# An S5 state scan with a fourth tree level, shared between VectorE and GpSimd, and its coefficients built later

## The chip, the cores and the metric

The kernel runs on one core of one Trainium2 chip. TensorE (PE) does the matrix products and transposes, VectorE (DVE), ScalarE (ACT) and GpSimd (POOL) work element by element, and SyncE (SP) issues the DMAs. The metric is the device time of one execution in microseconds: the median of several runs.

## The reference, cut to what matters

The program is a trunk of two layers over 2048 positions of width 1024. The even layer makes one projection and feeds stick-breaking attention and an S5 branch; the odd layer is a chunked gated linear attention. The change concerns the S5 branch and the two gate projections beside it:

```python
h = rms_norm(x, even_norm_g[i])
proj = h @ even_w_in[i]                      # q | k | v | gate A | S5 input u | gate B
...
lam_bar = jnp.exp(lam * dt)                  # 32 groups x 64 complex states
b_bar = ((lam_bar - 1.0) / lam)[..., None] * bmat
bu = lax.complex(jnp.einsum('gnp,blgp->blgn', b_bar.real, uf),
                 jnp.einsum('gnp,blgp->blgn', b_bar.imag, uf))
_, hstate = lax.associative_scan(combine, (a, bu), axis=1)   # h_t = lam_bar h_(t-1) + bu_t
y = (jnp.einsum('gpn,blgn->blgp', c_re, hstate.real)
     - jnp.einsum('gpn,blgn->blgp', c_im, hstate.imag) + d_skip * uf)
```

## The kernel before

All large products are made in two parts of reduced precision: `split` (L314 and L315) has ACT round a tile to `hi` and another engine take the rest, `lo`; each product is then three matmuls (`mm3`, L67 to L69). `sh` and `sl` are the parts of activations, `whi` and `wlo` those of weights.

The normalized and transposed input stands in four tiles hT0 to hT3 of 512 positions each (`m` = 0 to 3). `Norm.tiles` makes one tile of 128 positions: a sum of squares on ACT (L95), `nms` and `nrs` on POOL (L54, L56), `h` on DVE (L97), transposes on PE (`ntp`, L102), and copies to hT. The gate projections are sweeps over the four blocks (`first_gates`, `gates`): 96 matmuls of 512 columns a block into `gps`, then a sigmoid on ACT and a product on DVE into `sg` (L365). The PSUM ring that `gps` and `ups` share holds four tiles.

The S5 recurrence works on chunks of 8 positions, so that 256 chunks remain. Its coefficients are made once, in `s5_setup`: powers of lam_bar (`er`, L199 on POOL, then small DVE steps `p`), W by a chain of complex products (`cmul`, six instructions each, L228 to L233, on POOL), its transposes (L246) to `bin_d`; G by 8 `cmul`s that build on one another (on DVE); from G and `bz` the matrices K0 by 128 small matmuls (L290), copied to `kt` (L296, L297), reloaded as `ka` (8 DMAs, L302) and stored to `k0_d` (16 DMAs, L305), the DMAs all on SP's queue. `between(m)` runs between the blocks of the first gate sweep: norm tiles of the next block, and at m=1 `coefficients()`.

`s5_in` takes the 32 groups in two halves `cb`, each as 8 pairs of groups: for each `cb`, for two halves of the sequence and each of 8 offsets j, it splits hT with a stride of 8 elements (two splits of 128x512, `b` = 0 and 1), makes 24 matmuls of 256 columns into `ups`, and copies them to `U` (ACT, L487). Then it transposes U, multiplies by W (`bp`, L500) and copies the result to `H` (DVE, L504): 8 pairs x real and imaginary x 256 chunks for each `cb`. `scan_up` combines neighbours at distances 1, 2 and 4 with the powers `pwr` and `pwi` (three tree levels; `cplx_acc` is five instructions, `ca`, `cb` twice, `ca`, `H`, L458 to L462, on DVE), and then a chain of 31 steps of four POOL instructions of 128x16 (L530 to L533) runs over every eighth chunk. `scan_down` brings the results back down the tree. After `s5_in` comes the gate sweep of the next 512 columns (the "512 gates"), then `s5_out` (`yps`), and further gates.

Each engine works through its own queue in order. The order in which the queues are filled is set by a scheduler from the program and its dependencies, not by the text order alone, so the code's stages interleave on an engine.

Of the kernel before, what the change touches and what calls it, by code (L numbers as in the profile page):

```python
# [155 lines left out]
def s5_setup(e, room, lr, li, dt, sn, sh, b_re, b_im, c_re, c_im, dsk, bin_d, k0_d, co_d):

# [6 lines left out]
    V = nc.vector  # L164
    MU, AD, SU = ALU.mult, ALU.add, ALU.subtract

    e.pwr = [e.cst.tile([P, NI], F32, name=f"pwr{a}") for a in range(4)]
    e.pwi = [e.cst.tile([P, 2, NI], F32, name=f"pwi{a}") for a in range(4)]
    with e.pool("s5s", 1, "right") as s, e.pool("s5t", 2, "right") as s2, e.pool("s5w", 1, "right") as sw, \
            e.pool("s5p", 2, "right", PSUM) as pp:  # L170
        def tt(a, b, op, name):
# [38 lines left out]


        pr, pi = br, bi
        for a in range(6):
# [4 lines left out]
            if a >= 2:
                V.tensor_copy(e.pwr[a - 2], pr)
                V.tensor_scalar(e.pwi[a - 2][:, 0, :], pi, -1.0, None, MU)  # L220
                V.tensor_copy(e.pwi[a - 2][:, 1, :], pi)
# [37 lines left out]
                V.tensor_scalar(G[a][q, :, 0, :], ps[q].rearrange("q h (i r p) -> q (h i) r p", r=2, p=16)[:, :, r],  # L259
                                -1.0 if a else 1.0, None, MU)  # L260
# [189 lines left out]
def cplx_acc(e, tp, dst, src, lv, n, eng):  # L450

    nI = dst.shape[2]
    i0 = e.i0
    a = tp.tile([P, 2, nI, n], F32, tag="ca", name="ca")
    b = tp.tile([P, 2, nI, n], F32, tag="cb", name="cb")
# [2 lines left out]
    eng.tensor_tensor(a, src, pr, ALU.mult)  # L458
    for r in range(2):
        eng.tensor_tensor(b[:, r], src[:, 1 - r], pi[:, r].unsqueeze(2).to_broadcast([P, nI, n]), ALU.mult)  # L460
    eng.tensor_tensor(a, a, b, ALU.add)
    eng.tensor_tensor(dst, dst, a, ALU.add)  # L462


def s5_in(e, pn, hT, w_in, bin_d, u_d, H, lo_eng):

    nc, tc = e.nc, e.tc
    with e.pool("u_b", 2, "right") as ub, e.pool("u_1", 1, "right") as u1, e.pool("u_p", 2, "right", PSUM) as up:
        ws = pn.load(w_in, 4 * D, 512, lo_eng)
        for cb in range(2):  # L470
            nc.vector.memset(H[cb][:, :, :, 0:1], 0.0)
            bt = u1.tile([P, 2, 8, P], F32, tag="bt", name="bt")
            for a in range(2):
                nc.sync.dma_start(out=bt[:, a], in_=bin_d[a, cb * 8:cb * 8 + 8].rearrange("i j q -> j i q"))
            for half in range(2):
                U = ub.tile([P, 16, T8, 16], F32, tag="U", name="U")
                for j in range(T8):
                    hi = pn.s.tile([P, KD, P], F32R, tag="sh", name="sh")
                    lo = pn.s.tile([P, KD, P], F32R, tag="sl", name="sl")
                    for b in range(2):  # L480
                        split(nc, hi[:, :, b * 64:(b + 1) * 64], lo[:, :, b * 64:(b + 1) * 64],
                              hT[half * 2 + b][:, :, j::T8], lo_eng)
# [5 lines left out]
                for g4 in range(4):  # L488
# [8 lines left out]
                    for i in range(2):  # L497
                        for par in range(2):
                            for a in range(2):
                                nc.tensor.matmul(bp[par * 64:par * 64 + 64, a, i, :],  # L500
                                                 lhsT=bt[:, a, g4 * 2 + i, par * 64:par * 64 + 64],
                                                 rhs=us[:, i * 2 + par, :], start=True, stop=True)
                    i0 = g4 * 2
                    nc.vector.tensor_copy(H[cb][:, :, i0:i0 + 2, 1 + half * P:1 + (half + 1) * P], bp)  # L504
# [5 lines left out]
def scan_up(e, H, i1, tp, t2):  # L510

    B = H[:, :, :, 1:]
    V, G = e.nc.vector, e.nc.gpsimd
    for i0 in range(0, 8, 4):
        e.i0 = i1 + i0
        b = B[:, :, i0:i0 + 4]
        for h in range(2):
            c = slice(h * 128, h * 128 + 128)
            bh = b[:, :, :, c]
            cplx_acc(e, tp, bh[:, :, :, 1::2], bh[:, :, :, 0::2], 0, 64, V)  # L520
        cplx_acc(e, tp, b[:, :, :, 3::4], b[:, :, :, 1::4], 1, 64, V)
        cplx_acc(e, tp, b[:, :, :, 7::8], b[:, :, :, 3::8], 2, 32, V)
    ii = slice(i1, i1 + 8)
    pr = e.pwr[3][:, ii].unsqueeze(1).to_broadcast([P, 2, 8])
    pi = e.pwi[3][:, :, ii]
    for c in range(15, NC, 8):
        src = B[:, :, :, c - 8]
        a = t2.tile([P, 2, 8], F32, tag="sa", name="sa")
        b = t2.tile([P, 2, 8], F32, tag="sb", name="sb")
        G.tensor_tensor(a, src, pr, ALU.mult)  # L530
        G.tensor_tensor(b, src[:, ::-1], pi, ALU.mult)
# [1 line left out]
        G.tensor_tensor(B[:, :, :, c], B[:, :, :, c], a, ALU.add)  # L533


def scan_down(e, H, i1, tp):

    B = H[:, :, :, 1:]
    V = e.nc.vector
    for i0 in range(0, 8, 4):  # L540
        e.i0 = i1 + i0
        b = B[:, :, i0:i0 + 4]
        cplx_acc(e, tp, b[:, :, :, 11::8], b[:, :, :, 7:NC - 1:8], 2, 31, V)
        cplx_acc(e, tp, b[:, :, :, 5::4], b[:, :, :, 3:NC - 1:4], 1, 63, V)
        cplx_acc(e, tp, b[:, :, :, 2:128:2], b[:, :, :, 1:127:2], 0, 63, V)
        cplx_acc(e, tp, b[:, :, :, 128::2], b[:, :, :, 127:NC - 1:2], 0, 64, V)
# [686 lines left out]
def tile_trunk(ctx, tc, x, even_norm_g, even_w_in, sb_q_norm_g, sb_k_norm_g, s5_lambda_re, s5_lambda_im, s5_log_dt,  # L1233
# [17 lines left out]
    V, G = nc.vector, nc.gpsimd  # L1251

    def coefficients():
        s5_setup(e, room, *angles, s5_b_re[0], s5_b_im[0], s5_c_re[0], s5_c_im[0],
                 s5_d[0], bin_d, k0_d, co_d)

    with ExitStack() as st:
# [12 lines left out]
        first, angles, room = first_gates(e, pn, nrm, hT, w0, 3 * D, zs_d, lambda: s5_angles(  # L1270
            e, sap, s5_lambda_re[0], s5_lambda_im[0], s5_log_dt[0]))
# [5 lines left out]
        H = [hpool.tile([P, 2, 8, NC + 1], F32, name=f"H{cb}") for cb in range(2)]  # L1277
# [96 lines left out]
```

## Time and profile before

| | |
|---|---|
| median of 3 runs | 2872.51 us (2870.74 to 2874.99) |
| profiled execution | 2872.48 us, span of the core 2870.8 us |
| mean granted clock of PE | 0.989 |
| POOL busy | 1197.6 us (42%), 1321 instructions |
| HBM | 129.36 MB read, 74.65 MB written, 71 GB/s |

Times in the profile count from the start of the span. A row of a group of instructions gives line, engine, operation, `out<-in` with the shapes of both, the count, busy time and mean duration in ns, then the idle time of that engine just before these instructions and what ended it. A row of a timeline gives start, duration, engine, line and operation. A wait is put down to what ended it last.

Places in time: the first gate sweep with the norms and coefficients takes the first 150 us, `ups` of cb=0 and cb=1 run from 150 to 276 us, the 512 gates and the scan to about 395 us, the next gates and `yps` come behind.

### The profile page before, as it was taken

The numbers are of one execution on the slowest core, as the hardware profiler recorded it, in microseconds if no ns is written. First come the engines' busy times: TensorE is split into PE (matmuls) and PEld (weight loads), VectorE is DVE, ScalarE is ACT, GpSimd is POOL, SyncE is SP. The second block draws the span as 40 slices with busy tenths as digits, with TensorE's granted clock in tenths as the row PEclk, the third lists the DMA queues.
The fourth block names the chain that finished last, engine by engine and source line by source line (L and its number), as shares of the span: only waits on it lengthen the run. The fifth ranks groups of instructions, "written<-read, shape, count | busy, mean of one in ns | idle before, by whom it ended". The sixth has DMA issues, their size and how long they took to land.

```text
span 2870.8 us, 46525 instructions
## 1 busy us (share of the span) xinstructions
PE 2765.3 (96%) x17433; PEld 2496.6 (87%) x17433; DVE 1719.9 (60%) x2733; ACT 1365.0 (48%) x2988; POOL 1197.6 (42%) x1321
## 2 busy tenths in 40 slices
PE   6989979899999999999999999999999999999999
PEld 6788767889999999999899978887788999999887
DVE  7768965657676857685767783223345566565521
ACT  4576224446555655555555552223345566565310
POOL 7201821366665665666556730000023455455300
PEclk9999989999999999999999999999999999999999
DMA  5532136511110111111112124332131021121343
GB/s 170 153 81 75 58 94 201 173 44 43 29 41 27 45 29 40 29 41 27 41 27 73 58 72 143 104 103 86 56 99 41 31 67 54 36 78 60 125 137 114
DMA packets 246898, 215.69 MB, mean 75 GB/s; under 512 B 46256, under 2 KB 215568, under 8 KB 246160
## 3 DMA queue, kind: packets, MB, share of 16 engines
q1 hardware_dynamic: 246096, 210.62, 24.2%
q8 instruction: 137, 2.24, 0.3%
q10 hardware_dynamic: 576, 2.10, 0.2%
q14 instruction: 89, 0.73, 0.1%
HBM read 129.36 MB, written 74.65 MB: 71 GB/s over the span
## 4 chain that ended last, share of the span: by engine, by line
PE 78%; DVE 7%; POOL 4%; issue 4%; ACT 3%; DMA 3%; SPq 1%; ACTq 0%; POOLq 0%; DVEq 0%
PE av L807 6%; PE pp L68 6%; PE pp L67 6%; PE pp L69 6%; PE ops L69 5%; PE ops L68 5%; PE ops L67 5%; PE w L796 4%; PE gps L67 3%; PE gps L68 3%; PE gps L69 3%; PE qk L67 2%; PE qk L69 2%; PE qk L68 2%; PE z L68 2%
## 5 line engine op out<-in xcount | busy, mean ns | idle before, releaser
L719 POOL TENSOR_TENSOR sl<-hT,sh 128x1024 fp32r<-128x1024 f32 x128 | 322.2, 2518 | 343.0 <-ACT sh L718 304.8
L67 PE MATMUL pp<-whi,sh 128*128 128x384 f32 x1024 | 357.4, 349 | 0.7 <-ACT whi L314 0.6
L68 PE MATMUL pp<-wlo,sh 128*128 128x384 f32 x1024 | 351.1, 343 | 0.2
L69 PE MATMUL pp<-whi,sl 128*128 128x384 f32 x1024 | 348.0, 340 | 0.0
L790 DVE TENSOR_TENSOR_SCAN pt<-om,pt,zero 128x513 f32<-128x513 f32 x192 | 279.2, 1477 | 38.0 <-ACT om L788 37.3
L67 PE MATMUL gps<-sh,whi 128*128 128x512 f32 (+1 forms) x672 | 252.8, 389 | 23.1 <-DVE sg L365 20.3
L68 PE MATMUL gps<-sl,whi 128*128 128x512 f32 (+1 forms) x672 | 259.1, 386 | 3.5 <-DVE sl L315 3.5
L69 PE MATMUL gps<-sh,wlo 128*128 128x512 f32 (+1 forms) x672 | 256.5, 384 | 0.0
L799 DVE TENSOR_TENSOR tl<-w,th 128x512 fp32r<-128x512 f32 (+2 forms) x320 | 186.6, 599 | 95.5 <-ACT th L798 93.6
L798 ACT ACTIVATE th<-w 128x512 fp32r<-128x512 f32 (+2 forms) x320 | 163.9, 535 | 149.3 <-PE w L796 148.8
L315 DVE TENSOR_TENSOR sl<-hT,sh 128x1024 fp32r<-128x1024 f32 (+1 forms) x148 | 172.1, 1186 | 50.4 <-ACT sh L314 48.2
L69 PE MATMUL ops<-woh,ol 128*128 128x512 f32 x496 | 196.8, 397 | 0.7 <-DVE ol L315 0.7
L68 PEld LDWEIGHTS pp<-wlo,sh 128*128 128x128 f32 x1024 | 193.6, 189 | 3.8 <-POOL wlo L315 1.7
L67 PEld LDWEIGHTS pp<-whi,sh 128*128 128x128 f32 x1024 | 193.5, 189 | 3.6 <-ACT whi L314 1.3
L68 PE MATMUL ops<-wol,oh 128*128 128x512 f32 x496 | 196.2, 395 | 0.0
L67 PE MATMUL ops<-woh,oh 128*128 128x512 f32 x496 | 195.6, 395 | 0.0
L69 PEld LDWEIGHTS pp<-whi,sl 128*128 128x128 f32 x1024 | 193.3, 189 | 2.6
L790 DVE TENSOR_TENSOR_SCAN pt<-om,zero 128x129 f32<-128x129 f32 (+3 forms) x128 | 158.8, 1262 | 56.8 <-ACT om L788 56.2
L314 ACT ACTIVATE sh<-hT 128x1024 fp32r<-128x1024 f32 (+1 forms) x148 | 155.8, 1093 | 62.0 <-PE gps L69 32.5
L788 ACT ACTIVATE om<-z 128x512 f32<-128x512 f32 (+2 forms) x320 | 167.0, 538 | 37.6 <-PE z L784 22.7
L718 ACT ACTIVATE sh<-hT 128x1024 fp32r<-128x1024 f32 x128 | 135.5, 1059 | 90.8 <-PE pp L68 90.5
L796 PE MATMUL w<-ident,pt 128*128 128x128 f32 x1088 | 165.2, 273 | 8.6 <-DVE tl L799 6.0
(327 smaller groups left out, 8001.7 us busy)
## 6 DMA issues: line engine op xcount, KB each, us to landing
zs_d<-sg SPq DMA_DIRECT2D x80, 256.0 KB
o<-o_d SPq DMA_DIRECT2D x80, 256.0 KB
xt<-in_x_dram SPq DMA_DIRECT2D x28, 512.0 KB
r<-in_even_w_in_dram SPq DMA_DIRECT2D x64, 192.0 KB
zs<-zs_d SPq DMA_DIRECT2D x64, 128.0 KB
o_d<-ot SPq DMA_DIRECT2D x64, 128.0 KB
r<-in_odd_w_in_dram SPq DMA_DIRECT2D x64, 128.0 KB
zs<-zs_d SPq DMA_DIRECT2D x32, 256.0 KB
```

The costliest lines, as they stand in the source:

```text
L67: nc.tensor.matmul(out, lhsT=lhi, rhs=rhi, start=start, stop=False)
L68: nc.tensor.matmul(out, lhsT=lhi, rhs=rlo, start=False, stop=False)
L69: return nc.tensor.matmul(out, lhsT=llo, rhs=rhi, start=False, stop=stop)
L314: a = nc.scalar.activation(hi, src, AF.Copy)
L315: b = lo_eng.tensor_tensor(lo, src, hi.bitcast(F32), ALU.subtract)
L719: a = nc.gpsimd.tensor_tensor(sl, ht, sh.bitcast(F32), ALU.subtract)
L788: nc.scalar.activation(o[:, lo:512], z[:, :n], AF.Sigmoid, scale=-scale)
L790: nc.vector.tensor_tensor_scan(pt[:, lo:][:, ::-1], o[:, lo:][:, ::-1], zr.to_broadcast([P, n + 1]), 1.0 if prev[i] is None else prev[i], ...
L796: nc.tensor.transpose(w[:, s, :], pt[:, lo + s * P:lo + (s + 1) * P], e.ident)
L798: nc.scalar.activation(th[:, :ni, qs], w[:, :ni, :], AF.Copy)
L799: nc.vector.tensor_tensor(tl[:, :ni, qs], w[:, :ni, :], th[:, :ni, qs].bitcast(F32), ALU.subtract)
L807: nc.tensor.matmul(av[:, qs], lhsT=a[:, s, :], rhs=b[:, s, qs], start=diag and x == 0, stop=c == 0 and x == len(prods) - 1)
```

## The change

1. The coefficients are built at m=2 of the first gate sweep, behind the norm tiles of block 3, instead of at m=1, ahead of the norm tiles of block 2. The 8 products of G run on POOL instead of DVE.
2. In cb=1, half of the strided splits (16 of 32) run on POOL.
3. H is one tile of 16 pairs. The tree has a fourth level (distance 8). At each level DVE takes 6 of a cb's 8 pairs and POOL 2. The chain has 15 steps instead of 31, over all 16 pairs at once (128x32), after both up-sweeps.

DVE's scan instructions go from 160 to 140, POOL gets 100, and the chain goes from 248 POOL instructions to 60.

```diff
-    e.pwr = [e.cst.tile([P, NI], F32, name=f"pwr{a}") for a in range(4)]
+    e.pwr = [e.cst.tile([P, NI], F32, name=f"pwr{a}") for a in range(5)]
...
-        for a in range(6):
+        for a in range(7):
             r2 = tt(tt(pr, pr, MU, f"p1{a}"), tt(pi, pi, MU, f"p2{a}"), SU, f"p3{a}")
...
         for t in range(8):
-            cmul([G[a][:, :, t + 1, :] for a in range(2)], br, bi, G[0][:, :, t, :], G[1][:, :, t, :], 1, V)
+            cmul([G[a][:, :, t + 1, :] for a in range(2)], br, bi, G[0][:, :, t, :], G[1][:, :, t, :], 1, nc.gpsimd)
...
                     for b in range(2):
                         split(nc, hi[:, :, b * 64:(b + 1) * 64], lo[:, :, b * 64:(b + 1) * 64],
-                              hT[half * 2 + b][:, :, j::T8], lo_eng)
+                              hT[half * 2 + b][:, :, j::T8], nc.gpsimd if cb and b else lo_eng)
...
-            scan_up(e, H[cb], cb * 8, u1, ub)
+            scan_up(e, H, cb, u1)
+        scan_chain(e, H, ub)
         for cb in range(2):
-            scan_down(e, H[cb], cb * 8, u1)
+            scan_down(e, H, cb, u1)
...
+def scan_level(e, H, tp, cb, lv, dst, src):
     B = H[:, :, :, 1:]
+    i1 = cb * 8
+    w = (2, 3, 6, 6)[lv]
+    for i0, nI, eng in [(a, w, e.nc.vector) for a in range(0, 6, w)] + [
+            (a, 1 if lv == 0 else 2, e.nc.gpsimd) for a in ((6, 7) if lv == 0 else (6,))]:
+        i = slice(i1 + i0, i1 + i0 + nI)
+        cplx_acc(e, tp, B[:, :, i, dst], B[:, :, i, src], lv, i1 + i0, eng)
...
+def scan_up(e, H, cb, tp):
+    for lv in range(4):
+        s = 2 << lv
+        scan_level(e, H, tp, cb, lv, slice(s - 1, NC, s), slice(s // 2 - 1, NC, s))
...
+def scan_chain(e, H, t2):
+    B, G = H[:, :, :, 1:], e.nc.gpsimd
+    pr = e.pwr[4].unsqueeze(1).to_broadcast([P, 2, NI])
+    for c in range(31, NC, 16):
+        src = B[:, :, :, c - 16]
...
+def scan_down(e, H, cb, tp):
+    for lv in range(3, -1, -1):
+        s = 2 << lv
+        scan_level(e, H, tp, cb, lv, slice(s + s // 2 - 1, NC, s), slice(s - 1, NC - 1, s))
...
         def between(m):
-            if m == 1:
-                coefficients()
             if m < 3:
                 nrm.tiles(m * 4 + 4, m * 4 + 8)
+            if m == 2:
+                coefficients()
             return first
```

Three places where the queues change. Names carry buffer numbers; the line numbers of the changed kernel are one lower than those of the kernel before at the same code.

PE, before: the last K0 products (`ps<-G,bz`) and what follows.

```order
L290 MATMUL ps_1046<-G0_887,bz0_988 16x128
L290 MATMUL ps_1046<-G1_888,bz1_989 16x128
L290 MATMUL ps_1046<-G0_887,bz0_988 16x128
L290 MATMUL ps_1046<-G1_888,bz1_989 16x128
L67 MATMUL gps_1576<-sh_1565,whi_230 128x512
L68 MATMUL gps_1576<-sl_1566,whi_230 128x512
L69 MATMUL gps_1576<-sh_1565,wlo_231 128x512
L67 MATMUL gps_1573<-sh_1561,whi_226 128x512
```

PE in the changed kernel, the same place.

```order
L289 MATMUL ps_1368<-G0_1209,bz0_1310 16x128
L289 MATMUL ps_1368<-G1_1210,bz1_1311 16x128
L289 MATMUL ps_1368<-G0_1209,bz0_1310 16x128
L289 MATMUL ps_1368<-G1_1210,bz1_1311 16x128
L67 MATMUL ups_1780<-whi_1723,sh_1774 128x256
L68 MATMUL ups_1780<-wlo_1724,sh_1774 128x256
L69 MATMUL ups_1780<-whi_1723,sl_1775 128x256
L67 MATMUL ups_1780<-whi_1729,sh_1774 128x256
```

Before, m=3's gates (`gps`) still stand behind K0, about 12 us of them. Now all of them stand ahead of it, and the first `ups` follow directly.

POOL in the changed kernel: the end of the G products, the splits of cb=1 and the first scan step. Before, POOL had at this place the last norm's `nrs` and then the first chain's steps of 128x16.

```order
L231 TENSOR_TENSOR G0_1209<-cm0_1295,cm1_1296 128x16x16
L232 TENSOR_TENSOR G1_1210<-cm2_1297,cm3_1298 128x16x16
L314 TENSOR_TENSOR sl_2520<-hT1_88,sh_2519 128x8x64
L314 TENSOR_TENSOR sl_2552<-hT1_88,sh_2551 128x8x64
L314 TENSOR_TENSOR sl_2584<-hT1_88,sh_2583 128x8x64
L314 TENSOR_TENSOR sl_2616<-hT1_88,sh_2615 128x8x64
L314 TENSOR_TENSOR sl_2648<-hT1_88,sh_2647 128x8x64
L314 TENSOR_TENSOR sl_2680<-hT1_88,sh_2679 128x8x64
L314 TENSOR_TENSOR sl_2712<-hT1_88,sh_2711 128x8x64
L457 TENSOR_TENSOR ca_2452<-H_1711,pwr0_906 128x256
L459 TENSOR_TENSOR cb_2453<-H_1711,pwi0_911 128x128 x2
L460 TENSOR_TENSOR ca_2452<-ca_2452,cb_2453 128x256
```

The in-order queue of POOL now carries the splits that PE's `ups` of cb=1 need, and between them the scan steps of cb=0.

DVE, before, in the 512 gates: behind the weights of the next gates (`wlo`) the second cb's scan_down begins (`ca<-H1,pwr2`).

```order
L315 TENSOR_TENSOR sl_4623<-hT0_87,sh_4622 128x1024
L462 TENSOR_TENSOR H0_1697<-H0_1697,ca_3613 128x2x4x64
L315 TENSOR_TENSOR wlo_4595<-r_4592,whi_4594 128x512
L458 TENSOR_TENSOR ca_3620<-H1_1698,pwr2_600 128x248
L460 TENSOR_TENSOR cb_3621<-H1_1698,pwi2_604 128x124 x2
L461 TENSOR_TENSOR ca_3620<-ca_3620,cb_3621 128x248
L315 TENSOR_TENSOR wlo_4601<-r_4598,whi_4600 128x512
L462 TENSOR_TENSOR H1_1698<-H1_1698,ca_3620 128x2x4x31
```

DVE in the changed kernel: scan_down of the first cb begins (`ca<-H,pwr3`), and splits of hT3 for the last block of the 512 gates stand behind it.

```order
L364 TENSOR_TENSOR sg_3953<-sg_3953,gps_3850 128x512
L457 TENSOR_TENSOR ca_3350<-H_1711,pwr3_909 128x180
L459 TENSOR_TENSOR cb_3351<-H_1711,pwi3_914 128x90 x2
L460 TENSOR_TENSOR ca_3350<-ca_3350,cb_3351 128x180
L461 TENSOR_TENSOR H_1711<-H_1711,ca_3350 128x2x6x15
L457 TENSOR_TENSOR ca_3364<-H_1711,pwr2_908 128x372
L459 TENSOR_TENSOR cb_3365<-H_1711,pwi2_913 128x186 x2
L460 TENSOR_TENSOR ca_3364<-ca_3364,cb_3365 128x372
L461 TENSOR_TENSOR H_1711<-H_1711,ca_3364 128x2x6x31
L364 TENSOR_TENSOR sg_3957<-sg_3957,gps_3851 128x512
L457 TENSOR_TENSOR ca_3378<-H_1711,pwr1_907 128x378
L459 TENSOR_TENSOR cb_3379<-H_1711,pwi1_912 128x189 x2
```

Before, hT3's splits and the first cb's scan_down stood ahead of the row that waits for POOL's last chain; now the first row of scan_down waits for the only chain, and hT3's splits come behind it.

More of the change, by code (lines that the diff above doesn't have):

```diff
@@ L153, in s5_angles, with s5_setup @@
     return lr, li, dt, sn, sh
[L156 removed]
+def s5_setup(e, lr, li, dt, sn, sh, b_re, b_im, c_re, c_im, dsk, bin_d, k0_d, co_d):
     nc, tc = e.nc, e.tc
@@ L165, in s5_setup @@
     MU, AD, SU = ALU.mult, ALU.add, ALU.subtract
-    e.pwr = [e.cst.tile([P, NI], F32, name=f"pwr{a}") for a in range(4)]
-    e.pwi = [e.cst.tile([P, 2, NI], F32, name=f"pwi{a}") for a in range(4)]
+    e.pwr = [e.cst.tile([P, NI], F32, name=f"pwr{a}") for a in range(5)]
+    e.pwi = [e.cst.tile([P, 2, NI], F32, name=f"pwi{a}") for a in range(5)]
     with e.pool("s5s", 1, "right") as s, e.pool("s5t", 2, "right") as s2, e.pool("s5w", 1, "right") as sw, \
@@ L192, in s5_setup @@
         V.memset(two, 2.0)
-        x = room[:, 0:NI]
-        V.tensor_tensor(x, lr, dt, MU)
+        x = tt(lr, dt, MU, "x")
         V.tensor_scalar(x, x, LOG2E, None, MU)
@@ L416, in first_gates @@
     silu_out(e, pn, pss, 0, out_d, 0)
-    return ws, angles, rows[:, 3]
+    return ws, angles
 def gates(e, pn, hT, w, c0, out_d, row0, lo_eng, between=None, also=None, ws=None, sp=None, last=LAST):
@@ L447, in gates, with cplx_acc @@
     return out
[L450 to L455, printed above, removed]
+def cplx_acc(e, tp, dst, src, lv, i0, eng):
+    nI, n = dst.shape[2:]
+    g = "g" if eng is e.nc.gpsimd else "v"
+    a = tp.tile([P, 2, nI, n], F32, tag="ca" + g, name="ca")
+    b = tp.tile([P, 2, nI, n], F32, tag="cb" + g, name="cb")
     pr = e.pwr[lv][:, i0:i0 + nI].unsqueeze(1).unsqueeze(3).to_broadcast([P, 2, nI, n])
@@ L461, in cplx_acc @@
     eng.tensor_tensor(a, a, b, ALU.add)
-    eng.tensor_tensor(dst, dst, a, ALU.add)
+    return eng.tensor_tensor(dst, dst, a, ALU.add)
 def s5_in(e, pn, hT, w_in, bin_d, u_d, H, lo_eng):
@@ L469, in s5_in @@
         ws = pn.load(w_in, 4 * D, 512, lo_eng)
+        nc.vector.memset(H[:, :, :, 0:1], 0.0)
         for cb in range(2):
-            nc.vector.memset(H[cb][:, :, :, 0:1], 0.0)
             bt = u1.tile([P, 2, 8, P], F32, tag="bt", name="bt")
@@ L502, in s5_in @@
                                                  rhs=us[:, i * 2 + par, :], start=True, stop=True)
-                    i0 = g4 * 2
-                    nc.vector.tensor_copy(H[cb][:, :, i0:i0 + 2, 1 + half * P:1 + (half + 1) * P], bp)
-            scan_up(e, H[cb], cb * 8, u1, ub)
+                    i0 = cb * 8 + g4 * 2
+                    nc.vector.tensor_copy(H[:, :, i0:i0 + 2, 1 + half * P:1 + (half + 1) * P], bp)
+            scan_up(e, H, cb, u1)
+        scan_chain(e, H, ub)
         for cb in range(2):
-            scan_down(e, H[cb], cb * 8, u1)
@@ L510, in scan_up @@
-def scan_up(e, H, i1, tp, t2):
+            scan_down(e, H, cb, u1)
+def scan_level(e, H, tp, cb, lv, dst, src):
     B = H[:, :, :, 1:]
[L513 to L529, printed above, removed]
+    i1 = cb * 8
[4 more added lines that the diff above has]
+        cplx_acc(e, tp, B[:, :, i, dst], B[:, :, i, src], lv, i1 + i0, eng)
@@ L530, in scan_up @@
+def scan_up(e, H, cb, tp):
[7 more added lines that the diff above has]
+        src = B[:, :, :, c - 16]
+        a = t2.tile([P, 2, NI], F32, tag="sa", name="sa")
+        b = t2.tile([P, 2, NI], F32, tag="sb", name="sb")
         G.tensor_tensor(a, src, pr, ALU.mult)
-        G.tensor_tensor(b, src[:, ::-1], pi, ALU.mult)
+        G.tensor_tensor(b, src[:, ::-1], e.pwi[4], ALU.mult)
@@ L532, in scan_up @@
         G.tensor_tensor(a, a, b, ALU.add)
         G.tensor_tensor(B[:, :, :, c], B[:, :, :, c], a, ALU.add)
[L536 to L546, printed above, removed]
+def scan_down(e, H, cb, tp):
+    for lv in range(3, -1, -1):
+        s = 2 << lv
+        scan_level(e, H, tp, cb, lv, slice(s + s // 2 - 1, NC, s), slice(s - 1, NC - 1, s))
@@ L570, in s5_out @@
                             nc.tensor.matmul(pss[r][:, b], lhsT=Co[q, a, i, :],
-                                             rhs=H[ct // 2][q, a, ct % 2 * 4 + i, 0:NC], start=a == 0, stop=False)
+                                             rhs=H[q, a, ct * 4 + i, 0:NC], start=a == 0, stop=False)
                     for r in range(2):
@@ L1253, in coefficients @@
     def coefficients():
-        s5_setup(e, room, *angles, s5_b_re[0], s5_b_im[0], s5_c_re[0], s5_c_im[0],
+        s5_setup(e, *angles, s5_b_re[0], s5_b_im[0], s5_c_re[0], s5_c_im[0],
                  s5_d[0], bin_d, k0_d, co_d)
@@ L1263, in between @@
         def between(m):
-            if m == 1:
-                coefficients()
             if m < 3:
                 nrm.tiles(m * 4 + 4, m * 4 + 8)
+            if m == 2:
+                coefficients()
             return first
-        first, angles, room = first_gates(e, pn, nrm, hT, w0, 3 * D, zs_d, lambda: s5_angles(
+        first, angles = first_gates(e, pn, nrm, hT, w0, 3 * D, zs_d, lambda: s5_angles(
             e, sap, s5_lambda_re[0], s5_lambda_im[0], s5_log_dt[0]))
@@ L1276, in tile_trunk @@
         hpool = sr.enter_context(e.pool("Hp", 1, "right"))
-        H = [hpool.tile([P, 2, 8, NC + 1], F32, name=f"H{cb}") for cb in range(2)]
+        H = hpool.tile([P, 2, NI, NC + 1], F32, name="H")
         s5_in(e, pn, hT, w0, bin_d, u_d, H, V)
```

## The prediction

> **What bounds the kernel now.** I read the page's busy shares first, then the span cut into stretches by windows, then PE's waits up to 530 us, and last the timelines at the places where those waits fall. The first line is the page's; the columns of the others are: stretch, length, busy time and instructions of PE, weight loads, DVE, ACT and POOL, then granted PE clock, DMA share and GB/s.
>
> ```profile
> PE 2765.3 (96%) x17433; PEld 2496.6 (87%) x17433; DVE 1719.9 (60%) x2733; ACT 1365.0 (48%) x2988; POOL 1197.6 (42%) x1321
> 60.00:135.00 75.00, 71.20 (x375) 59.00 (x377) 56.56 (x94) 34.08 (x52) 26.53 (x37) 0.97 0.43 130
> 135.00:171.00 36.00, 27.69 (x257) 25.09 (x247) 17.67 (x29) 21.53 (x29) 0.00 (x0) 0.91 0.80 165
> 211.00:276.00 65.00, 60.25 (x547) 58.80 (x546) 59.17 (x80) 42.94 (x57) 4.65 (x6) 0.95 0.17 50
> 276.00:355.00 79.00, 75.83 (x380) 61.79 (x378) 68.01 (x105) 25.36 (x35) 68.50 (x161) 0.98 0.23 77
> 355.00:418.00 63.00, 45.35 (x196) 36.68 (x197) 45.52 (x74) 15.40 (x21) 24.23 (x83) 0.86 0.25 77
> ```
>
> PE is busy 96% of the span, and the change only touches the first 420 us or so; afterwards both kernels issue the same work in the same order. So the time is that of PE plus its stalls, and what counts is which stalls of the first 420 us go and which come. PE idles 8.3 us in 135–171 (36.00 less 27.69) and 17.7 us in 355–418, and in 211–276 PE (60.25 of 65) and DVE (59.17) are both nearly full: there DVE has no slack to give. The waits by name (engine and line that waited, what for: total, times, longest):
>
> ```profile
> PE gps L67 <- DVE sg L365: 20.3, 4, 17.0
> PE bp L500 <- DVE H L504: 4.7, 1, 4.7
> PE ups L67 <- ACT whi L314: 3.4, 1, 3.4
> PE ups L67 <- ACT U L487: 2.1, 1, 2.1
> 394.14 0.80 PE L67 MATMUL gps<-sh,whi 128*128 128x512 f32 x1 [16.98 <-DVE sg L365]
> L458 DVE TENSOR_TENSOR ca<-H,pwr 128x248 f32<-128x248 f32 x4 | 2.4, 610 | 16.5 <-POOL H L533 16.5
> ```
>
> The one large stall, 17.0 us, ends at 394.14; the last row says why DVE was late with sg: its own queue stood 16.5 us for the last chain step on POOL (H of L533). That is what the shorter chain is aimed at.
>
> **POOL and DVE exclude each other.** Everything below hangs on this, since the change moves three kinds of work to POOL. Timeline rows (start, length, engine, line):
>
> ```profile
> 59.76 4.76 DVE L315 TENSOR_TENSOR sl<-hT,sh 128x1024 fp32r<-128x1024 f32 x3
> 60.28 1.60 POOL L229 TENSOR_TENSOR cm<-W,bi 128x256 f32<-128x256 f32 x1
> 61.85 1.60 POOL L230 TENSOR_TENSOR cm<-W,br 128x256 f32<-128x256 f32 x1
> 63.41 1.60 POOL L231 TENSOR_TENSOR cm<-W,bi 128x256 f32<-128x256 f32 x1
> 65.05 1.21 DVE L315 TENSOR_TENSOR sl<-hT,sh 128x1024 fp32r<-128x1024 f32 x1
> 363.48 1.20 POOL L531 TENSOR_TENSOR sb<-H,pwi 128x16 f32<-128x16 f32 x1
> 366.02 0.23 POOL L530 TENSOR_TENSOR sa<-H,pwr 128x16 f32<-128x16 f32 x1
> 367.11 0.23 POOL L530 TENSOR_TENSOR sa<-H,pwr 128x16 f32<-128x16 f32 x1
> L229 POOL TENSOR_TENSOR cm<-B,fi 128x256 f32<-128x256 f32 x1 | 0.6, 616 | 0.0
> L232 POOL TENSOR_TENSOR bb<-cm,cm 128x256 f32<-128x256 f32 x1 | 0.7, 737 | 0.0
> ```
>
> A split `sl` alone takes 1.21 us on DVE and a 128x256 product alone 0.62 on POOL. Side by side, three splits take 4.76 (1.59 each) and the products 1.60 each: one product waits for one split and the reverse. 3 x 1.21 + 2 x 0.62 is 4.87, so the two engines take turns and nothing overlaps. At 363.48 a 128x16 step that takes 0.23 alone takes 1.20 behind a split. So where both have such work, I add their times. The Trainium skill ("SBUF — State Buffer", Who interferes with whom) says the same: a DVE operation with two SBUF inputs and a POOL operation that reads SBUF share one port pair, and the later one fully blocks; by that rule nothing that moves to POOL is free while DVE has such operations. The trace agrees, by these rows.
>
> **Edit 1: coefficients later, G loop on POOL.** Rows for it:
>
> ```profile
> 105.10 1.74 DVE L259 TENSOR_SCALAR G<-ps 64x256 f32<-64x256 f32 x4
> L231 DVE TENSOR_TENSOR cm<-G,bi 128x256 f32<-128x256 f32 x8 | 3.3, 418 | 0.0
> L315 DVE TENSOR_TENSOR wlo<-r,whi 128x512 fp32r<-128x512 f32 x24 | 16.5, 695 | 5.0 <-ACT whi L314 4.9
> L315 DVE TENSOR_TENSOR sl<-hT,sh 128x512 fp32r<-128x512 f32 x72 | 76.9, 1100 | 20.3 <-ACT sh L314 20.2
> 134.41 0.86 PE L290 MATMUL ps<-G,bz 128*16 128x128 f32 x23
> 138.06 0.50 PE L67 MATMUL gps<-sh,whi 128*128 128x512 f32 x1
> 150.01 0.58 PE L67 MATMUL ups<-whi,sh 128*128 128x256 f32 x1 [2.80 <-DVE sg L365]
> 158.34 5.40 SPq L305 DMA_DIRECT2D k_d<-ka  x5
> 166.94 0.38 ACT L487 ACTIVATE U<-ups 128x256 f32<-128x256 f32 x1 [1.22 <-DMA k_d<-ka]
> 168.91 0.28 PE L67 MATMUL ups<-whi,sh 128*128 128x256 f32 x1
> 169.03 0.28 PE L68 MATMUL ups<-wlo,sh 128*128 128x256 f32 x1
> ```
>
> Before, G is filled at 105–107 and DVE runs the 48 instructions (0.42 us each, 20 us) between other things, so that PE starts the K0 products at 134.41 without waiting. After, they are POOL's: 8 x (4 x 0.62 + 2 x 0.74) is 31.7 us alone, some 30 when issued back to back. The four norm tiles ahead of G's transposes put its start at about 113. In that stretch the order gives DVE 4 splits of 1024 (1.2 each), 8 `wlo` (0.7) and 8 splits of 128x512 (1.1) that m=3's gates and the first two `ups` need: 19 us of exclusion, some 18 at pitch. So G ends at 143 (nothing overlaps with it) to 161 (all of it in turns). PE reaches K0 at about 143: 150, where its `ups` start before, less the 3.5 us of K0 products (134.41 to 138.06, where m=3's gates go on), less the 2.8 us stall there. PE waits 0 to 18 there.
>
> What follows is a fixed chain: kt copies, ka loads, 16 k_d stores, and then the copy of U, whose buffer lies where the setup's tiles lay and so waits for all stores (166.94, from 134.41: 32.5; 31.5 after, since no weight loads stand among the stores). Before, PE covers that with 12 us left of m=3 and four `ups`; after, only four `ups` (24 products each, at a pitch of 0.12, 2.9 us) are ahead. U comes at 143+31.5 = 174.5 to 192.5 against 166.94: +8 to +26. The rows at 59.76 say that turns are taken, so I take +20. The whi and U stalls (3.4, 2.1) go, but into this wait, which is longer. At the start the order also puts `er` (4 of 1.07 us) ahead of the norms' small POOL steps and brings the W chain forward: I take −1, between −4 and +3.
>
> **Edit 2: half the splits of cb=1 on POOL, with scan_up of cb=0 (211–276).** The nearest rows:
>
> ```profile
> L315 POOL TENSOR_TENSOR gwl<-r,gwh 128x512 fp32r<-128x512 f32 x3 | 4.0, 1380 | 21.2 <-ACT gwh L314 21.2
> L460 DVE TENSOR_TENSOR cb<-H,pwi 128x256 f32<-128x256 f32 (+3 forms) x64 | 27.0, 461 | 0.1
> L462 DVE TENSOR_TENSOR H<-H,ca 128x512 f32<-128x512 f32 (+3 forms) x32 | 25.1, 785 | 0.7
> L458 DVE TENSOR_TENSOR ca<-H,pwr 128x512 f32<-128x512 f32 (+3 forms) x32 | 24.7, 772 | 16.9 <-POOL H L533 16.5
> L461 DVE TENSOR_TENSOR ca<-ca,cb 128x512 f32<-128x512 f32 (+3 forms) x32 | 20.2, 631 | 0.4
> ```
>
> The last four rows sum to 97 us, some 88 when issued back to back (the start of one lies up to 0.1 before the end of the last): 22 for one pass over one cb. A quarter less, one more level and fewer calls make it 18 on DVE. The quarter on POOL has no row. POOL's plain 128x512 is 1.3–1.4, twice DVE's 0.69, so by elements it is 11.6 us; 15 if strides cost it as they cost DVE. A strided split on POOL has none either: bounds 1.3 (plain rows) and 2.4 (times DVE's own 1.10 to 0.60 for strided against plain). I take 1.6, nearer the plain row, because POOL is slower by element already and so has more time for each access.
>
> Before, exclusive work is 32 splits of 1.05 plus 22, 55.6 of 65 us. After, DVE has 16.8 + 18, POOL 16 x 1.6 = 25.6 plus 13: 73.4 in turns, +18. The 9.4 us that DVE spends on copies out of PSUM (H, L504) can now lie beside POOL; of them I credit 8. So +10. Bounds: if nothing excludes, PE's own 60.25 remains, −5; with 2.4 and 15 and no credit, 88.2, +32. A rule of the Trainium skill ("GPSIMD Engine Reference", Performance pitfalls for Q7 kernels) says that inner steps over 8 bytes cost POOL half as much again; 16 splits of 1.9 would make this term +15. No POOL row here is strided.
>
> **Edit 3: one chain of 15 for all pairs, scan_down in turns (276 to 418).** The second chain's first and last instructions of 31 x 4:
>
> ```profile
> 331.03 0.23 POOL L530 TENSOR_TENSOR sa<-H,pwr 128x16 f32<-128x16 f32 x1 [1.17 <-DVE H L462]
> 383.68 0.41 POOL L533 TENSOR_TENSOR H<-H,sa 128x16 f32<-128x16 f32 x1
> ```
>
> Before, it takes 53.1 us for 31 steps (pitch 1.09 alone, by the rows at 366.02 and 367.11), and lets DVE go at 382, 106 us behind the end of `ups` at 276. After, it starts when both up-sweeps are done, again some 55 us after `ups` end, and takes 15 steps of twice the width: 1.2 (alone) to 1.5, 18–23 us. So it ends near 78 us behind `ups`, 28 us earlier, and the 16.5 us wait goes. But DVE's scan_down of both cbs (36), 12 splits of 1.13 (13.6), 8 `wlo` of 0.6 (4.8) and POOL's quarter (25 to 31) must now take turns: 79 to 86 us behind the chain, where before DVE ran ahead on cb=0 during the chain. The next gates' second block starts at 157 to 164 against 142 (418 less 276). Since PSUM-fed `sg` lies beside POOL, I take +13, between −17 (only the wait goes) and +20.
>
> **Sum.** −1 + 20 + 10 + 13 = +42. The profiled execution took 2872.48 (span 2870.8), the median is 2872.51, so the sum stands against both: 2914. Off the first 420 us I change nothing.
>
> **Rivals.** *Faster*: POOL's share truly lies beside DVE. Then G ends at PE's arrival and U costs +8 less the 5.5 of whi and U stalls, +3; cb=1 gains 5; the 17 us chain wait and its slow clock (0.86 in 355–418) go. 2872.5 + 3 − 5 − 17 = 2853. It decides if POOL products beside splits average under 0.9 us; the rows at 60–64 speak against it, the chain wait speaks for it. *Even*: exclusion holds in edit 1 (+20), while cb=1 stays at +0 and the chain's 17 us go entirely: 2875. *Worse*: strided POOL work costs the upper bound: −1 + 23 + 32 + 20 = +74, 2946; against it, POOL is bound by its lanes rather than by access.
>
> **Chances.** Forecast 0.50, worse 0.15, even 0.12, faster 0.23. A change below 0.2% (5.7 us) can't be told from none in this kernel. From the cases: faster 0.23, same 0.09 (most of the even case), slower 0.68. The range takes the faster case's 2853 and the worse case's 2946 with little beyond; the forecast's own is 2890 to 2935.
>
> **What would show it.** Right: PE stands 15–25 us before K0 or the fifth `ups`; POOL's G products average 0.9–1.0 us; 16 POOL splits show 2 us or more beside DVE; PE is idle over 10 us in cb=1; the 16.5 us wait for L533 is gone but `gps` still waits 15 us or so for `sl` or `sg`. Wrong: G done by 145, cb=1 at 65 us or less, or no stall after the chain.

## The result, and the profile after

| | before | after |
|---|---|---|
| median | 2871.86 us (2870.74 to 2874.99, 4 runs) | 2911.41 us (2905.78 to 2912.22, 4 runs) |
| profiled execution: span | 2870.8 us | 2904.0 us |
| mean granted clock of PE | 0.989 | 0.983 |

The changed kernel is slower: ratio 1.0132, 95% interval [1.0114, 1.0149]. The forecast was 2914 us. The profiled execution is the fastest of the four (2905.78).

The same windows as in the prediction, of the kernel after (stretch, length, busy time of PE, weight loads, DVE, ACT, POOL, granted clock, DMA share, GB/s):

```profile
60.00:135.00 75.00, 68.98 (x347) 56.80 (x347) 44.94 (x48) 37.94 (x58) 39.76 (x52) 0.98 0.45 141
135.00:171.00 36.00, 24.56 (x237) 21.63 (x236) 21.51 (x28) 19.87 (x27) 27.27 (x31) 0.81 0.44 127
171.00:211.00 40.00, 21.48 (x159) 21.27 (x159) 14.76 (x15) 17.16 (x22) 0.00 (x0) 0.74 0.42 67
276.00:355.00 79.00, 66.64 (x443) 58.40 (x444) 59.32 (x71) 27.20 (x40) 33.21 (x34) 0.89 0.20 61
355.00:418.00 63.00, 53.46 (x211) 42.16 (x210) 47.86 (x69) 16.91 (x21) 43.72 (x96) 0.86 0.23 72
```

PE now idles 11.4 us in 135–171 and 18.5 in 171–211. PE's longest waits up to 560 us, from the same view as before:

```profile
PE ups L67 <- ACT U L486: 18.5, 1, 18.5
PE ntp L102 <- DVE h L97: 16.1, 4, 9.6
PE ps L289 <- POOL G L231: 11.4, 1, 11.4
PE gps L67 <- DVE sg L364: 10.1, 4, 3.1
PE bp L499 <- DVE H L503: 10.0, 1, 10.0
PE gps L68 <- DVE sl L314: 5.4, 5, 2.9
```

The 17.0 us stall for `sg` is gone (its longest is 3.1). In its place stand a wait for the G products on POOL, one for U, and one twice as long for the copies of H (10.0 instead of 4.7). The wait of the transposes `ntp` lies in the first 75 us; before it is 12.3. Three marks on PE's timeline show where the time came from: the `ups` behind a `bp` in the second half of cb=0, the first `gps` of the 512 gates, and the same block of `yps` behind the scan. The first three rows are of before, the other three of after:

```profile
196.98 0.39 PE L69 MATMUL ups<-whi,sl 128*128 128x256 f32 x1
275.61 0.40 PE L67 MATMUL gps<-sh,whi 128*128 128x512 f32 x1
452.04 0.49 PE L570 MATMUL yps<-H,Co 64*128 64x256 f32 x2
```

```profile
223.44 0.38 PE L69 MATMUL ups<-whi,sl 128*128 128x256 f32 x1
313.51 0.40 PE L67 MATMUL gps<-sh,whi 128*128 128x512 f32 x1
489.65 0.49 PE L570 MATMUL yps<-H,Co 64*128 64x256 f32 x2
```

So the part up to the first mark takes 26.5 us more, the part with cb=1 90.1 us instead of 78.6 (+11.4), and the part with the chain and scan_down 176.1 instead of 176.4. I use these three parts below and call them I, II and III. The marks differ by 37.6 us at the third, but the spans by 33.2: 4.4 us are given back behind it. They come from the end of the program; another 2.1 are lost between the third mark and there. From the `kt` rows below to the end of the span, PE issues the same 4656 matmuls in the same order in both kernels, in 667.7 us before and 661.3 after. The second row of each pair is a window of 150 us in which PE is never idle and runs at full clock: 648 matmuls before, 654 after. First before, then after:

```profile
2203.02 0.38 PE L1189 MATMUL kt<-ident,k 128*128 128x128 f32 x2
2710.00:2860.00 150.00, 150.00 (x648) 121.45 (x647) 35.25 (x53) 15.51 (x25) 0.00 (x0) 1.00 0.45 145
```

```profile
2242.78 0.38 PE L1189 MATMUL kt<-ident,k 128*128 128x128 f32 x2
2743.30:2893.30 150.00, 150.00 (x654) 122.49 (x653) 36.38 (x55) 15.81 (x25) 0.00 (x0) 1.00 0.46 146
```

This goes with edit 3: in the eleven traces with it the same stretch takes 659.7 to 661.5 us, in the three without it 667.7 to 671.5. The change doesn't touch the code there, and no run shows why these matmuls follow each other faster.

### The profile page after: what moved, and what is told of

Same layout as the page of the kernel before. It is cut to its first block, busy times and chain, and to the rows that moved or that the text cites. A ratio compares the mean times of both kernels' runs of the same rounds, so it can differ in the third digit from the quotient of the medians.

```text
span 2904.0 us, 46470 instructions
## 1 busy us (share of the span) xinstructions
PE 2771.8 (95%) x17433; PEld 2499.9 (86%) x17433; DVE 1709.7 (59%) x2655; ACT 1368.5 (47%) x2988; POOL 1275.0 (44%) x1297
## 4 chain that ended last, share of the span: by engine, by line
PE 79%; DVE 8%; POOL 4%; ACT 3%; issue 3%; DMA 2%; SPq 1%; ACTq 0%; DVEq 0%; POOLq 0%
PE av L807 6%; PE pp L67 5%; PE pp L68 5%; PE pp L69 5%; PE ops L69 5%; PE ops L67 5%; PE ops L68 5%; PE gps L67 4%; PE gps L68 4%; PE gps L69 4%; PE w L796 3%; PE qk L67 2%; PE qk L69 2%; PE qk L68 2%; PE pv L68 2%
## 5 line engine op out<-in xcount | busy, mean ns | idle before, releaser
L790 DVE TENSOR_TENSOR_SCAN pt<-om,pt,zero 128x513 f32<-128x513 f32 x192 | 279.0, 1476 | 38.3 <-ACT om L788 37.5
L314 DVE TENSOR_TENSOR sl<-hT,sh 128x1024 fp32r<-128x1024 f32 (+1 forms) x132 | 162.7, 1254 | 78.0 <-ACT sh L313 76.0
```

The source lines that it names most:

```text
L314: b = lo_eng.tensor_tensor(lo, src, hi.bitcast(F32), ALU.subtract)
L790: nc.vector.tensor_tensor_scan(pt[:, lo:][:, ::-1], o[:, lo:][:, ::-1], zr.to_broadcast([P, n + 1]), 1.0 if prev[i] is None else prev[i], ...
```

## The experiments

All ratios are against the kernel before on the same chip, with the 95% interval. The parts are read at the same three marks, each from one profiled execution; those of before are from one trace. "Early start" means that x, a small tile of the setup, is put back where the kernel before has it (explained below). The profiled execution of the changed kernel is 5.6 us below its median, so differences against it come out larger by the ratios than by the parts; and with edit 3 a ratio holds the 6 to 8 us of the last stretch, which the parts do not.

| kernel | ratio | I to | II | III |
|---|---|---|---|---|
| before | 1 | 197.0 | 78.6 | 176.4 |
| after | 1.0132 [1.0114, 1.0149] | 223.4 | 90.1 | 176.1 |
| edit 1 on before | 1.0082 [1.0067, 1.0098] | 223.4 | 78.3 | 176.0 |
| late coefficients on before | 1.0057 [1.0042, 1.0072] | 217.2 | 78.7 | 176.4 |
| early coefficients in after | 1.0054 [1.0038, 1.0071] | 211.5 | 88.9 | 175.0 |
| G on DVE in after | 1.0088 [1.0073, 1.0103] | 214.8 | 89.5 | 176.0 |
| edits 2 and 3 | 1.0043 [1.0027, 1.0060] | 206.7 | 89.3 | 174.8 |
| edit 3 only | 1.0029 [1.0018, 1.0039] | 205.3 | 85.0 | 174.5 |
| splits on POOL, tree on DVE | 1.0014 [1.0004, 1.0023] | 204.6 | 89.1 | 167.2 |
| tree on DVE, chain of 15 | 0.9989 [0.9980, 0.9998] | 204.1 | 79.3 | 166.9 |
| two stores in after | 1.0071 [1.0056, 1.0087] | 210.9 | 90.1 | 176.6 |
| edit 3, early start | 1.0004 [0.9995, 1.0013] | 198.0 | 85.1 | 175.1 |
| tree on DVE, early start | 0.9943 [0.9931, 0.9956] | 196.7 | 79.3 | 167.1 |
| stores on POOL's queue | 0.9981 [0.9971, 0.9990] | 202.1 | 81.1 | 167.4 |

### Edit 1: what is late, and what is slow

Four kernels set the place of the coefficients and the engine of G, each on one side.

Edit 1 on the kernel before (with x in a tile of its own, as the change has it):

```diff
-            cmul(..., G[0][:, :, t, :], G[1][:, :, t, :], 1, V)
+            cmul(..., G[0][:, :, t, :], G[1][:, :, t, :], 1, nc.gpsimd)
...
-            if m == 1:
-                coefficients()
             if m < 3:
                 nrm.tiles(m * 4 + 4, m * 4 + 8)
+            if m == 2:
+                coefficients()
```

> The kernel before with edit 1 alone: coefficients at m=2 and the G products on POOL. Theory T (edit 1 makes PE wait for K0 and then for U, 26 us by the marks of the two traces): some 2898 us, with a K0 wait near 11 us and a U wait near 18. Rival R1 (the loss comes from the scan sharing POOL, and what is lost ahead of it is taken back by slack later): within 6 us of 2872.

Measured: +23.5 us (0.82% of 2872), K0 wait 11.4, U wait 19.2. Part I ends where it ends in the changed kernel (223.4), and parts II and III are those of before. R1 falls: nothing is taken back later.

The second `if` alone, with G left on DVE:

> The kernel before with the coefficients at m=2, the G products left on DVE. Theory T (two costs: POOL's slow G, 11 us, and the place of K0 behind all gates, which leaves only four ups to cover the stores to k_d): no K0 wait, a U wait of 15 to 20 us, some 2885 us. Rival R2 (the place costs nothing, only POOL's G does): within 6 us of 2872.

Measured: +16.4 us, no K0 wait. But the U wait is not 15 to 20, it is longer than with G on POOL:

```profile
187.76 0.58 PE L67 MATMUL ups<-whi,sh 128*128 128x256 f32 x1 [24.18 <-ACT U L486]
```

So the late place of the coefficients costs most of edit 1. Both of these kernels also give x its own tile, which costs some 7 us where the coefficients are early (below). No run has late coefficients with x in its old place, but here the first `ups` starts at 151.8 us, against 150.0 before, so at this point at most 2 us of that are left. POOL's G adds 7 us, not its 11.4 of K0 wait: what PE waits less for G it waits more for U.

The reverse, in the changed kernel:

```diff
+            if m == 1:
+                coefficients()
             if m < 3:
                 nrm.tiles(m * 4 + 4, m * 4 + 8)
-            if m == 2:
-                coefficients()
```

> The changed kernel with the coefficients back at m=1, the G products still on POOL. Theory T: the place's share of 13 to 15 us is given back, some POOL cost stays: 2893 to 2900 us, U wait under 8 us. Rival R2 (only POOL's G costs): 2905 to 2911, with a K0 wait as before.

Measured: 22 us back by the ratios (1.0132 to 1.0054), somewhat more than T had, and 14.3 by the third mark, 12 of them in part I; a K0 wait of 5.2 and no U wait among the long ones; `ups` wait 9.6 us for `sg` instead, of which more below. R2 falls.

> The changed kernel with the G products back on DVE, coefficients still at m=2. Theory T: the K0 wait of 11.4 us goes and the U wait of 18.5 us stays: some 2900 us. Rival R2 (only POOL's G costs): both waits go, 2885 us.

Measured: 13 us back by the ratios, 9.4 by the third mark. The K0 wait is gone and the U wait is 24.0, as on the kernel before. T's size holds; its U wait of 18.5 grew by the half of what K0 gave back.

Why does U come so late? In the kernel after, this is the line of work (PE's K0, SP's second lot of stores, ACT's copy of U, the first `ups` behind it):

```profile
157.95 2.40 PE L289 MATMUL ps<-G,bz 128*16 128x128 f32 x31 [11.44 <-POOL G L231]
174.58 7.13 SPq L304 DMA_DIRECT2D k_d<-ka  x8
184.56 7.12 SPq L304 DMA_DIRECT2D k_d<-ka  x8
193.88 1.21 ACT L486 ACTIVATE U<-ups 128x256 f32<-128x256 f32 x4 [16.02 <-DMA k_d<-ka]
194.32 0.58 PE L67 MATMUL ups<-whi,sh 128*128 128x256 f32 x1 [18.52 <-ACT U L486]
```

From K0 to U it takes 35.9 us, of which the stores' issue is 14.3. To see whether the stores are on the path, 14 of them are left out, so that most of `k0_d` is not filled:

```diff
-            for j in range(8):
+            for j in range(1):
                 nc.sync.dma_start(out=k0_d[h * 16:h * 16 + 16, ...], in_=ka...)
```

> The changed kernel with 14 of the 16 stores to k_d left out (most of K0 then stays zero). Theory T (the late coefficients cost because U's buffer waits for K0, kt, ka and the 16 stores in a row): the K0 wait of 11 us stays, the U wait of 18.5 shrinks by 12 to 15: some 2897 us. Rival R6 (U is held by something else of that stage): above 2906.

Measured: the K0 wait stays at 11.4, the U wait falls to 7.4, and the ratio to 1.0071, 17.5 us less than the changed kernel (12.5 in part I). R6 falls.

```profile
181.74 0.58 PE L67 MATMUL ups<-whi,sh 128*128 128x256 f32 x1 [7.36 <-ACT U L486]
```

### Edits 2 and 3: the shared scan

> The changed kernel without edit 1: coefficients at m=1, G on DVE; POOL's splits of cb=1, POOL's quarter of the scan and the chain of 15 steps stay. Theory T (stage by stage: cb=1 costs 11 us more by the marks, the stage of the chain and scan_down comes out even): 2883 us. Rival R3 (the cb=1 loss is only what a late start of the stage makes of it): within 6 us of 2872.

Measured: +12.3 us. Part II is 89.3, though it starts 16.7 us earlier than in the changed kernel; and with edit 1 alone it starts as late as there and takes 78.3. So it is not the late start that makes it long (R3 falls). Part I is not that of before, though, which T had not foreseen: it ends at 206.7, 9.7 us late. I come back to it.

The splits of cb=1 back on DVE as well:

```diff
-                              hT[half * 2 + b][:, :, j::T8], nc.gpsimd if cb and b else lo_eng)
+                              hT[half * 2 + b][:, :, j::T8], lo_eng)
```

> The changed kernel without edits 1 and 2: all strided splits on DVE, POOL's quarter of the scan and the chain of 15 steps stay. Theory T (all work of both engines counts in turns): in cb=1 DVE has 33.6 + 18 and POOL 13, 64.6 against 55.6 before, +1 to +9 with the copies from PSUM beside it: 2873 to 2881 us. Rival R4 (POOL's strided splits alone cost the 11 us): 2872 or less.

Measured: +8.3 us; part II is 85.0, 6.4 above before. POOL's quarter of the tree is enough to make part II longer, and the total is in the range of T; R4 falls.

The other half: splits on POOL, the whole tree on DVE.

```diff
-    w = (2, 3, 6, 6)[lv]
-    for i0, nI, eng in [(a, w, e.nc.vector) for a in range(0, 6, w)] + [
-            (a, 1 if lv == 0 else 2, e.nc.gpsimd) for a in ((6, 7) if lv == 0 else (6,))]:
+    w = (2, 4, 8, 8)[lv]
+    for i0, nI, eng in [(a, w, e.nc.vector) for a in range(0, 8, w)]:
```

> The changed kernel without edit 1, POOL's splits of cb=1 kept, the whole tree on DVE (8 pairs a level), the chain of 15 steps on POOL. Theory T: in cb=1 DVE has 16.8 + 24 and POOL 29, some +6; behind it scan_down has no POOL partner and the 17 us wait for the chain shrinks: 2863 to 2872 us. Rival R5 (POOL's quarter is what pays for the chain's gain: DVE alone is the bound of scan_down): 2880 or more.

Measured: +4.0 us, above T's range and below R5's. Part II is 89.1 (+10.5, T had +6), part III 167.2, 9 us shorter than before. Part I's 7.6 us, which neither theory had, are in the total.

And both changes, so that POOL has only the chain:

> The fourth tree level and the chain of 15 steps alone: coefficients at m=1, G, all splits and the whole tree on DVE. Theory T (the chain of 31 steps made a 17 us stall, and sharing with POOL ate the gain): cb=1 +2, the stage behind it some 10 to 17 us shorter: 2857 to 2864 us. Rival R5 (DVE's own work bounds that stage): within 6 us of 2872.

Measured: −3.2 us. By the total alone that is R5's number. By the parts it is not: part III is 166.9, 9.5 us shorter than before, though DVE has a third more tree work there than in the changed kernel, and part II is 79.3. The gain is hidden by part I, 7 us late here too. Together the four kernels give: the short chain is worth 9 to 10 us in part III, and POOL's quarter takes some 8 of them back (174.5 and 174.8 with it, 166.9 and 167.2 without). In part II, against the kernel with neither (79.3), the quarter alone costs 5.7, the splits alone 9.8 and both together 10.0. So once POOL has the splits, its quarter costs part II next to nothing more; R4 was wrong that the quarter is free, but not far off about the splits.

### Where part I went in these kernels

The kernels with early coefficients still ended part I 7 to 15 us late. SP's queue and ACT's waits between 130 and 165 us show a part of it (tree on DVE with the chain of 15; then the same kernel with x in hT2's fourth row again):

```profile
142.97 7.42 SPq L304 DMA_DIRECT2D k_d<-ka  x8
152.49 1.00 SPq L338 DMA_DIRECT2D r<-in_even_w_in_dram  x2
ACT whi L313 <- DMA r<-in_even_w_in_dram: 14.0, 3, 8.2
```

```profile
126.84 4.55 SPq L339 DMA_DIRECT2D r<-in_even_w_in_dram  x3
136.88 3.55 SPq L339 DMA_DIRECT2D r<-in_even_w_in_dram  x1
146.31 7.32 SPq L305 DMA_DIRECT2D k_d<-ka  x8
ACT whi L314 <- DMA r<-in_even_w_in_dram: 1.6, 2, 0.9
```

With x in a tile of its own the scheduler takes another order at the start, and weight loads (`r`) that `ups` need stand behind eight stores; ACT waits 14.0 us for them, and with it the `sg` that PE waits for. In the second kernel four of these loads are ahead of the stores. The `sg` wait at the first `ups` is 8.5 us in the first kernel and 2.8 in the second. That is not all: the gates ahead of it start later too (first `gps` at 25.4 against 18.7 us) and end 4.7 us later. The edit that takes both back (`room` is the fourth row of hT2):

```diff
-        x = tt(lr, dt, MU, "x")
+        x = room[:, 0:NI]
+        V.tensor_tensor(x, lr, dt, MU)
```

> Edit 3 alone as before, but with x back in hT2's fourth row, as the kernel before has it, so that the first 150 us are those of the kernel before. Theory T (9 of the 8.7 us by which edit 3 alone was slower are the start's order that x's own tile lets the scheduler take; the scan itself costs 6 us in cb=1 and gives 2 back): 2873 to 2877 us. Rival R7 (x's tile means nothing): 2881.

Measured: 1.0004 [0.9995, 1.0013], even; 6 to 7 us less than without the edit. R7 falls. So edit 3 as the change has it is neither gain nor loss in the total. By the marks it is 6.2 us late at the third, and the faster matmuls of the last stretch give that back.

> The tree on DVE with the chain of 15 steps, and x back in hT2's fourth row. Theory T (the start's order costs 7 to 9 us, SP's weights standing behind the stores to k_d): 2860 to 2864 us, faster than the kernel before by 8 to 12. Rival R7 (x's tile means nothing): 2870.

Measured: 2860.26 us, 0.9943 [0.9931, 0.9956], 16.4 us faster than the kernel before by the ratio, 14.3 by the medians. Part I ends at 196.7 and part III is 167.1: 8.9 us are gained up to the third mark, and another 6.5 in the last stretch (661.2 instead of 667.7). This is the fastest version that was run.

> The version before this one with the 16 stores to k_d issued on POOL's queue, which is empty there, so that SP's weight loads for ups do not stand behind them. Theory T (SP's queue holds the weights): the whi wait of 3.4 us goes, 2856 to 2861 us. Rival R8 (the stores are slower from POOL, and U waits for them): 2866 or more.

Measured: 0.9981 [0.9971, 0.9990]; still faster than before, but 8 us slower by the medians than the version it was made from. The whi wait is gone and U is hardly later (a wait of 2.4 instead of 1.4), so neither theory describes it. Part I ends 5.4 us later, with PE waiting for `sg` a second time:

```profile
PE ups L67 <- DVE sg L365: 7.3, 2, 4.5
```

Why this `sg` comes late with the stores on that queue was not tried and stays open. ACT's 6.5 us wait for the stores of earlier `sg` tiles does not tell: the version it was made from has one of 6.7.

## Why the prediction came out right, step by step

The sum was 42 us, the marks give 37.6 at the third, the ratio 37.9. That it fits so well is partly luck: the term of edit 1 was too small by 7.5, that of edit 3 too large by 13, and the rest of the program, put at nothing, gave 4.4 back.

**Edit 1: +20 (and −1 for the start); measured +26.5, U being 27 us later, at 193.88.** POOL's G products were slowed as said, though not all of them ran in turns. The first starts at 119.00, the step that releases K0 ends at 157.90; seven `cmul`s take 38.9 us where seven take 26 at POOL's own pace. Groups of POOL:

```profile
119.00 0.62 POOL L227 TENSOR_TENSOR cm<-G,br 128x256 f32<-128x256 f32 x1 [15.16 <-DVE G L258]
157.18 0.72 POOL L231 TENSOR_TENSOR G<-cm,cm 128x256 f32<-128x256 f32 x1
L231 POOL TENSOR_TENSOR G<-cm,cm 128x256 f32<-128x256 f32 x8 | 8.8, 1105 | 0.0
L228 POOL TENSOR_TENSOR cm<-G,bi 128x256 f32<-128x256 f32 x8 | 6.1, 763 | 0.0
```

All six groups sum to 45 us for 48 instructions, 0.94 each, inside the 0.9 to 1.0 that was named as the sign. The K0 wait of 11.4 lies in 0 to 18. What was mis-sized is the chain from K0 to U, taken as 31.5 from 134.41 to 166.94: it measured 35.9, and 40 with G on DVE (146.83 to 186.74, where the first `ups` after the wait start). What is longer lies ahead of the first store to k_d: 16.6 us from K0's start, where it was 11.8 before. There K0's 128 products took 6.1 us instead of 3.7, and SP's queue was still issuing stores of `sg` until 168.8, just ahead of the ka loads. And the prediction laid the wait mostly on POOL's turns, while the runs put 16 of the 23 us on the late place with G on DVE (12 of 26.5, by part I, where G stays on POOL).

**Edit 2: +10; measured +11.4 for part II.** The size was right. The strided POOL split was taken as 1.6 us and measured 1.81 on average. The gain of 5 us that the faster rival had here did not occur.

```profile
L314 POOL TENSOR_TENSOR sl<-hT,sh 128x512 fp32r<-128x512 f32 x16 | 28.9, 1808 | 90.8 <-ACT sh L313 83.3 <-DVE sl L314 7.5
```

The sum in turns is not how the loss came about, though. In the first 53 us of part II POOL did 30.6 us of work, and PE was busy 50 of them; the loss lies in the last 37.5 us, mostly in PE's 10.0 us wait for H behind DVE's queue:

```profile
223.44:276.00 52.56, 50.13 (x447) 49.15 (x445) 38.34 (x39) 40.09 (x50) 30.64 (x24) 1.00 0.18 51
276.00:313.51 37.51, 26.48 (x215) 25.51 (x215) 28.26 (x30) 13.01 (x19) 18.85 (x18) 0.77 0.05 16
```

And splits and quarter cost 9.8 and 5.7 alone and 10.0 together, so the two shares do not add, as the sum had them do. That the size fits is in part luck.

**Edit 3: +13; measured −0.3 for part III.** This step failed. The chain came out nearly as worked out: it starts at 364.80 and ends at 389.0, 24.2 us where 18 to 23 were given, and DVE waits 6.5 us for it instead of 16.5.

```profile
DVE ca L457 <- POOL H L539: 6.5, 1, 6.5
389.00:455.50 66.50, 52.84 (x206) 41.33 (x206) 65.20 (x91) 16.88 (x23) 37.52 (x46) 0.85 0.22 70
```

Behind it I had added DVE's 54 us and all of POOL's 25 to 31 to 79–86. The second block of the next gates starts after 66.5 (455.5), 142 us behind the end of `ups`, as before. DVE is busy 98% of these 66.5, so it is the bound, but POOL's share did not delay it by its whole length. Its price by experiment is some 8 us (part III of 175 with it, 167 without), where it has 25 to 31 us of work. The direction was right, that sharing eats what the chain gives; the size was too large by 13.

**The rivals.** *Even* had edit 1 as the forecast had it, but cb=1 costs 11.4 and not nothing, and nothing is left of the chain's 17. *Faster* needed POOL's work to lie beside DVE's at no cost; no run shows a gain from that, and the kernel becomes faster when the work goes back to DVE. *Worse* needed dear strided work on POOL, which measured 1.81 and not 2.4. That 2.4 took DVE's plain 128x512 split as 0.60; the row shown has 0.695, which gives 2.1. And no run shows whether POOL is bound by its lanes, the reason given against this case.

**The signs.** POOL's products at 0.94, the U wait of 18.5, PE idle 13.5 us in part II and the end of the 16.5 us wait came as named. The 16 splits did not reach 2 us on average, and the `gps` waits for `sg` and `sl` sum to 15.5 but none is over 3.1.

**The rest of the program** was put at nothing, since both kernels issue the same work in the same order there. They do, and yet the last 4656 matmuls take 6.5 us less; the cause is open.

**Not in the prediction,** nor in the list of the change: x gets a tile of its own, and that changes the order of the first 150 us. In the kernels with late coefficients little of it is left when `ups` start; in those with early coefficients it costs 7 us of part I (205.3 to 198.0 and 204.1 to 196.7 when taken back).

## What to carry to other kernels

Before work moves from VectorE to GpSimd, price each instruction that reads SBUF on both as waiting for one of the other, as the rows at 59.76 showed, and remember that the price then came out between next to nothing and the whole of what was moved. Before a stage is put later, follow its results to the last thing that waits for them, reuse of memory included: here a buffer that waited for sixteen stores cost more than the slow engine. Put the two parts of a change on trial apart: the shorter chain was worth 9 us in its stage, and a quarter of the tree on GpSimd took 8 of them back there and up to 6 more in the stage before. And compare the stretches that a change does not touch as well: here one of them was 6.5 us shorter.

## What the runs showed of the hardware

- A strided split (128x512, step of 8 elements) on POOL took 1.53 to 1.73 us where DVE ran no more beside it than a copy out of PSUM or the end of a split; plain ones of that shape have a median of 1.31. So the step costs POOL a sixth to a third, where DVE's own splits go from 0.69 to 1.10. The Trainium skill ("GPSIMD Engine Reference", Performance pitfalls for Q7 kernels) has half as much again for reads with such a step; these rows have less.

```profile
246.44 1.53 POOL L314 TENSOR_TENSOR sl<-hT,sh 128x512 fp32r<-128x512 f32 x1 [1.98 <-DVE sl L314]
L314 POOL TENSOR_TENSOR gwl<-r,gwh x36: 1276/1308/2297, 559.2 to 2598.4; 128x512 fp32r<-128x512 f32 x36
```

- SP issues the stores to k_d at some 0.9 us each (7.1 us for 8, single ones 0.3 to 1.5), so sixteen of them hold back whatever stands behind them on the queue by 14 us.
- The same matmuls in the same order, at full clock and without a wait, ran at two paces: 648 in 150 us in the kernel before, 654 in the changed one. All eleven traces with edit 3 have the faster pace in their last 660 us.
